# Three small groups of fp32 matrix products moved to sub-tiles of the systolic array, in a decoder layer on one core

## The chip, the cores and the metric

The kernel runs on one core of one Trainium2 chip. TensorE multiplies matrices (in the profile PE for the products and PEld for the loading of their stationary operand, the weights), VectorE (DVE), ScalarE (ACT) and GpSimd (POOL) do elementwise work, SyncE (SP) issues most of the transfers. SBUF is the on-chip memory with 128 partitions; products land in PSUM, from where VectorE and ScalarE fetch them. The metric is the device time of one execution in microseconds; lower is better.

## The reference, cut to what matters

One decoder layer on 256 tokens of width 2048, all in float32: a projection feeds a gated DeltaNet (8 heads of 128) and an attention branch (8 heads); both are merged, projected, and followed by a gated feed-forward of width 5632. The change touches the DeltaNet:

```python
h = rms_norm(x, ln1[l])
proj = h @ w_in[l]
qkv_a, beta_a, decay_a, z_a, ... = split_columns(proj)
...
q = l2norm(q.reshape(shp))        # x * rsqrt(sum(x * x) + 1e-6)
...
beta = jax.nn.sigmoid(beta_logit)
g = -jnp.exp(a_log) * jax.nn.softplus(a_logit + dt_bias)
...
a_mat = jnp.where(strict, jnp.einsum('bhncd,bhnsd->bhncs', kb, k) * gamma, 0.0)
t_mat = lax.linalg.triangular_solve(eye + a_mat, eye, left_side=True, lower=True, unit_diagonal=True)
u = jnp.einsum('bhncs,bhnsv->bhncv', t_mat, v * beta[..., None])
```

Three things in it matter here: the 16 columns of the projection that give `beta_a` and `decay_a` (called gate columns below), the sum of squares of q over the head, and the inverse `t_mat` of a unit lower triangular matrix. The kernel takes chunks of 128 tokens instead of 64, which gives the same function.

## The kernel before, in words

All large products run on TensorE as a stream of 128x128 weights times 256 or 512 columns: `main_mm` (L98) issues them, `load_w` fetches a block of weights and splits it into a high and a low part of type fp32r with one cast on ScalarE (L108) and one subtraction on VectorE (L105). In order, the projections are q, k and v of the DeltaNet (`ps_gdn`), its output gate (`ps_z`), v of the attention (`ps_v`), q and k of the attention (`ps_moba`), the branch gates (`ps_gate`), then the branch outputs, the output projection, up and down.

Everything else is background work, written as Python generators in the list `bg`. `main_mm` counts up estimated nanoseconds, and each time they pass `EVERY` = 1700 it calls `tick()` (L90), which takes every generator one `yield` further. So a `yield` in the code stands for about 1.7 us of projections between two steps. A scheduler that simulates the engines then fixes the order of the instructions on each engine; each engine works through its own list in order. PSUM has three buffers for projections and five (`sdt`, tag "sd") for the background.

The touched places:

- *Gate columns* (L299 to L310). The weights `wbd` (128 x 16 columns of 16) are split into a high part in columns 0 to 15 and a low part in columns 32 to 47 of `wb2`; the gap is cleared by GpSimd. The normalised input stands in two fp32r parts `hh`, `hl`, so 16 x 2 products of 48 weight columns by 256 tokens add up in `ps_bd`. Rows 0 to 15 and 32 to 47 are then added to `z0`.
- *Sums of squares of q* (L497 to L501, in `gdn_pair`, which runs four times, for two heads each time). GpSimd squares q into `sq`. For two heads and two halves of the tokens, a product has `sq` as weights and one column of `ones` as stream, so that the sums land as columns, one lane per token. VectorE adds epsilon, scales, and writes row 0 of `st` (`S(0)`), which is read at the end of the unit (L659).
- *Inverse by doubling* (L596 to L627, in `gdn_unit`, twice, for 8 matrices of 128x128 each). First the 32x32 diagonal blocks are inverted on VectorE, into `TL` and, transposed, into `U`. Then two levels, w = 32 and w = 64, join neighbouring blocks: Y = (off-diagonal block of A) x (inverse of the upper block), then the new off-diagonal block of the inverse is -(inverse of the lower block) x Y. Each level does this with full 128x128 products: 8 of them (`py`) with the whole of `ats[p]` as weights and 64 columns as stream, a multiplication on VectorE with a 0/1 mask `my` into the even column blocks of Y, whose odd column blocks GpSimd had cleared, then 8 products (`pu`), and a subtraction from U on VectorE. A yield stands after the clearing of Y, after the mask, and after the subtraction.

An fp32 product is written as one `pe.matmul` and shows as two matmuls in the profile.

Of the kernel before, what the change touches and what calls it, by code (L numbers as in the profile page):

```python
# [11 lines left out]
F32 = mybir.dt.float32  # L12
F32R = mybir.dt.float32r
I32 = mybir.dt.int32
AF = mybir.ActivationFunctionType
ALU = mybir.AluOpType
# [3 lines left out]
P = 128  # L20
T = 256
D = 2048
KD = D // P
# [4 lines left out]
EPS = 1e-6  # L28
# [1 line left out]
SHIFT = 72  # L30
ATT_SCALE = 128 ** -0.5
CONST_FIELDS = [
    ("ident", 128), ("nm", 128), ("my", 2 * 64), ("nm3", 3 * 128), ("invf", 16),
]


def const_array():
    c = {}
    i = np.arange(P)
    c["ident"] = np.eye(P)  # L40
    c["nm"] = np.where(i[None, :] >= i[:, None], 0.0, -30000.0)
    my = np.zeros((P, 2, 64))
    for j in range(2):
        m = 32 << j
        e = i[(i // m) % 2 == 0][None, :]
        my[:, j, :] = (i[:, None] // (2 * m) == e // (2 * m)) & ((i[:, None] // m) % 2 == 1)
    c["my"] = my
    nm3 = np.zeros((P, 3, P))
    nm3[:, 1:, :] = np.where(i[None, :] <= i[:, None], 0.0, -1e30)[:, None, :]
    c["nm3"] = nm3  # L50
    inv = np.float32(500000.0) ** (-np.arange(16, dtype=np.float32) / np.float32(16))
    c["invf"] = np.broadcast_to(inv, (P, 16))
    return np.concatenate([c[n].reshape(P, -1) for n, _ in CONST_FIELDS], axis=1).astype(np.float32)
# [17 lines left out]
def layer_kernel(ctx: ExitStack, tc: tile.TileContext, xT, pos, cst, ceye, vec, convw, ffw, bdv,  # L71
                 w_gdn, w_z, w_bd, w_moba, w_mv, w_gate, w_ba, w_bb, w_o, w_up, w_dn, fnorm, out):
    nc = tc.nc
    pe, act, dve, pool, sp = nc.tensor, nc.scalar, nc.vector, nc.gpsimd, nc.sync
# [5 lines left out]
    def r3(t, b):  # L80
        return t.rearrange("p (a b) -> p a b", b=b)

    def mmg(ps, pairs, start=True, stop=True, **kw):
        n = len(pairs)
        for i, (a, b) in enumerate(pairs):
            pe.matmul(ps, a, b, start=(start and i == 0), stop=(stop and i == n - 1), **kw)  # L86
# [17 lines left out]
    def low(hi, lo, src, eng=None):  # L104
        return (eng or dve).tensor_tensor(lo, src, hi.bitcast(F32), op=ALU.subtract)  # L105
# [29 lines left out]
    ln1v, ln2v, gnv = vc[:, 0:16], vc[:, 16:32], vc[:, 32:33]  # L135
    ones = keep.tile([P, P + 96], F32, name="ones")[:, :P]
# [20 lines left out]
    def sdt(name):  # L157
        return pst[1].tile([P, 512], F32, name=name, tag="sd")
# [58 lines left out]
    def rstd(parts, tp, name):  # L217
        ps = sdt(name)[:, :T]
        mmg(ps, [(ones, t) for t in parts])
        r = tp.tile([P, T], F32, name=name)  # L220
        act.activation(r, ps, AF.Sqrt, bias=epst, scale=1.0 / D)
        dve.reciprocal(r, r)
        return r
# [7 lines left out]
    hh, hl = hc[:, :, 0, :], hc[:, :, 1, :]  # L231
# [3 lines left out]
    g = n1.enter_context(tc.tile_pool(name="n1", bufs=1, side="right"))  # L235

    xs = g.tile([P, KD, T], F32, name="xs")
# [15 lines left out]
    for k0, n in steps:  # L253
        s = slice(k0, k0 + n)
        for b in range(2):
            w = r3(wq[b], P)[:, s]
# [9 lines left out]
    wbd = g.tile([P, KD, 16], F32, name="wbd")  # L266
# [8 lines left out]
    C, o = {}, 0  # L275
# [1 line left out]
        C[n] = ct[:, o:o + s]  # L277
        o += s
    ident, nm = C["ident"], C["nm"]
    my = r3(C["my"], 64)  # L280
    eye = fk.tile([P, 8, 32], F32, name="eye")
    sp.dma_start(eye, ceye)

# [3 lines left out]
    sq = []  # L287
# [8 lines left out]
    dve.tensor_tensor(sq[0][:, 0], sq[0][:, 0], sq[0][:, 1], op=ALU.add)  # L296


    wb2 = g.tile([P, KD, 48], F32R, name="wb2")  # L299
    pool.memset(wb2.bitcast(F32), 0.0)  # L300
    act.copy(wb2[:, :, 0:16], wbd)
    low(wb2[:, :, 0:16], wb2[:, :, 32:48], wbd)
    s = sdt("ps_bd")[:48, :T]
    mmg(s, [(wb2[:, k, :], x_[:, k, :]) for k in range(KD) for x_ in (hh, hl)])
    R1 = rstd([sq[0][:, 0, :]], fk, "R1")
    R1b = both(R1)
    beta = fk.tile([16, T], F32, name="beta")
    z0 = fk.tile([16, T], F32, name="z0")
    act.copy(z0, s[32:48, :])
    dve.tensor_tensor(z0, z0, s[:16, :], op=ALU.add)  # L310
    ea = fk.tile([16, 1], F32, name="ea")
    gc = fk.tile([16, T], F32, name="gc")
    rem = fk.tile([16, P], F32, name="rem")
# [9 lines left out]
    m = m_st.enter_context(tc.tile_pool(name="m", bufs=2, reuse_waits="tile"))  # L323
    gdn_st, gu_st = ExitStack(), ExitStack()
    dr = gu_st.enter_context(tc.tile_pool(name="dr", bufs=2, space=bass.MemoryType.DRAM))
    gu = gu_st.enter_context(tc.tile_pool(name="gu", bufs=1, reuse_waits="tile"))
    g = gdn_st.enter_context(tc.tile_pool(name="g", bufs=2, side="right", reuse_waits="tile"))
# [124 lines left out]
    def wait(n):  # L452
        for _ in range(n):
            yield
# [17 lines left out]
    def gdn_pair(u, pr, kq, v):  # L472
# [9 lines left out]
        sq = g.tile([P, 2, T], F32, name="sqq", tag="un", bufs=1)  # L482
# [11 lines left out]
        def S(r):  # L494
            return st[:, r, 4 * pr:4 * pr + 4]

        pq = r3(sdt("ssq")[:, :4], 1)  # L497
        for i in range(2):
            for j in range(2):
                pe.matmul(pq[:, 2 * i + j], sq[:, j, i * P:(i + 1) * P], ones[:, :1], start=True, stop=True)  # L500
        dve.tensor_scalar(S(0), pq[:, :, 0], EPS, P * EPS, op0=ALU.add, op1=ALU.mult)  # L501

        pg = u["gB"][:, 2 * pr:2 * pr + 2, :]
        gam = g.tile([P, 2, 3, P], F32, name="gam", bufs=1)
        for j in range(2):
            c = 8 + hs[j]
            dve.scalar_tensor_tensor(gam[:, j, 0, :], pg[:, j, :P], cols[:, 0, c:c + 1], nm,
                                     op0=ALU.subtract, op1=ALU.min)
            dve.tensor_scalar(gam[:, j, 1, :], pg[:, j, P:], cols[:, 2, c:c + 1], 0.0, op0=ALU.add, op1=ALU.min)
            dve.scalar_tensor_tensor(gam[:, j, 2, :], pg[:, j, P:], cols[:, 1, c:c + 1], nm,  # L510
                                     op0=ALU.subtract, op1=ALU.min)
        act.activation(gam, gam, AF.Exp)
        yield

        kqh = g.tile([P, 2, 2, T], F32R, name="kqh", bufs=1)
        kql = g.tile([P, 2, 2, T], F32R, name="kql", bufs=1)
# [10 lines left out]
        jk = g.tile([P, P], F32, name="jk", bufs=1)  # L527
# [8 lines left out]
        for j in range(2):  # L536
            h, e = 2 * pr + j, 4 * pr + j
# [3 lines left out]
        for j in range(2):  # L541
            h, e = 2 * pr + j, 4 * pr + 2 + j
# [4 lines left out]
        for i in range(2):  # L547
            for k in range(4):
                b = slice(32 * k, 32 * k + 32)
# [9 lines left out]
        if pr:  # L559
            yield from gdn_unit(u)  # L560

    def gdn_unit(u):
# [4 lines left out]
        ats = [aq[:, 0, 2 * a + j, 2 * i, :] for a in range(2) for i in range(2) for j in range(2)]  # L567

        def half(t, i):
            return t.rearrange("p (a i j) c -> p i a (j c)", i=2, j=2)[:, i]  # L570


        N = gu.tile([P, 32, 32], F32, name="N", tag="Y", bufs=1)
        pool.dma_start(N.rearrange("p m c -> p (m c)"), bass.AP(tensor=dN.tensor, offset=dN.offset, ap=[[1024, 32], [0, 4], [1, 1024]]))
# [15 lines left out]
        TL = gu.tile([P, 8, P], F32, name="TL", tag="u", bufs=1)  # L590
        pool.dma_start(TL, dT[:, :P].rearrange("p s c -> s p c"))
        yield from wait(12)
        U = gu.tile([P, 8, P], F32, name="U", tag="U", bufs=1)
        with tc.issue_after(lows[-1].ins):
            dve.transpose(U.rearrange("p a b -> p (a b)"), TL.rearrange("p a b -> p (a b)"))
        for lv in range(2):  # L596
            w = 32 << lv

            def even(t):
                return t.rearrange("p a (b c d) -> p a b c d", c=2, d=w)[:, :, :, 0, :]  # L600

            def odd(t):
                return t.rearrange("p a (b c d) -> p a b c d", c=2, d=w)[:, :, :, 1, :]

            if lv == 0:
                Tm = even(TL)
            else:

                t21 = gu.tile([32, 8, 32], F32, name="t21", tag="Tm", bufs=1)
                dve.transpose(t21, U[:32, :, 32:64])  # L610
                pool.dma_start(TL[32:64, :, :32], t21)
                yield from wait(2)
                Tm = TL[:, :, :64]
            Y = gu.tile([P, 8, P], F32, name="Y", tag="Y", bufs=1)
            pool.memset(odd(Y), 0.0)
            yield
            py = sdt("py").rearrange("p (a b) -> p a b", a=8)
            for p in range(8):
                pe.matmul(py[:, p], ats[p], Tm[:, p], start=True, stop=True)  # L619
            dve.tensor_tensor(even(Y), py.rearrange("p a (b d) -> p a b d", d=w),  # L620
                              my[:, lv:lv + 1, :].rearrange("p a (b d) -> p a b d", d=w).to_broadcast([P, 8, 64 // w, w]), op=ALU.mult)
            yield
            pu = sdt("pu").rearrange("p (a b) -> p a b", a=8)
            for p in range(8):
                pe.matmul(pu[:, p], Y[:, p, :], odd(U)[:, p], start=True, stop=True)  # L625
            dve.tensor_tensor(odd(U), odd(U), pu.rearrange("p a (b d) -> p a b d", d=w), op=ALU.subtract)
            yield  # L627
        x = gu.tile([P, 8, P], F32, name="x", tag="u", bufs=1)
        pairs = [(2 * a + j, 4 * a + j) for a in range(2) for j in range(2)]
# [24 lines left out]
        act.copy(half(ot, 1), po.rearrange("p (a j) c -> p a (j c)", j=2))  # L654
        so = gu.tile([P, 8, P], F32, name="so", tag="Y", bufs=1)
        pool.tensor_tensor(so, ot, ot, op=ALU.mult)
# [9 lines left out]
        for p in range(8):  # L666
            dve.scalar_tensor_tensor(o2[:, p // 4 * 4 + p % 2 * 2 + p // 2 % 2, :], ot[:, p, :], st[:, 7, p:p + 1], zv[:, p, :],
                                     op0=ALU.mult, op1=ALU.mult)
        done.add(("out", u["n"]))
        yield from turn(zv, o2.rearrange("p a c -> p (a c)"), gu.tile([P, 8, P], F32, name="ox", tag="Y", bufs=1), sp, 4, 1)  # L670
        yield from wait(2)
# [113 lines left out]
    for n in range(2):  # L785
# [6 lines left out]
        for a in range(2):  # L792
            ps = by_token(w_moba[8 * n + 4 * a:8 * n + 4 * a + 4], hc, KD, "ps_moba")
            t = (m if a else mq).tile([P, 4, 2, P], F32, name=f"qk{a}", bufs=1)
# [27 lines left out]
    for t, nm_ in ((ya, "a"), (yb, "b")):  # L822
        yc.append(yp.tile([P, H, 2, T], F32R, name="yc" + nm_))
        for i in range(4):
            s = slice(2 * i, 2 * i + 2)
# [6 lines left out]
    m = m_st.enter_context(tc.tile_pool(name="mp", bufs=1, reuse_waits="tile"))  # L832
# [53 lines left out]
    b = bp.enter_context(tc.tile_pool(name="b", bufs=2, reuse_waits="tile"))  # L886
    sqa = b.tile([P, 2, T], F32, name="sqa", bufs=1)
    h2 = hp.tile([P, KD, 2, T], F32R, name="h2", tag="hc")
    for c in range(8):
# [10 lines left out]
        if c % 2 == 0:  # L900
            s = slice(2 * c, 2 * c + 4)
# [7 lines left out]
        else:  # L909
            sq = b.tile([P, 2, T], F32, name="sq2")  # L910
# [14 lines left out]
    b = bk.enter_context(tc.tile_pool(name="b2", bufs=2, reuse_waits="tile"))  # L925
# [69 lines left out]
    for k in range(NF):  # L995
        last = k >= NF - LAST
        ab = LAST if last else 2
        if k == NF - LAST:
# [3 lines left out]
            b = bk.enter_context(tc.tile_pool(name="b3", bufs=2, reuse_waits="tile"))  # L1002
# [102 lines left out]
```

## Time and profile before

| | us |
|---|---|
| median of three timed runs | 1457.8 (1457.72 to 1457.9) |
| profiled execution, whole | 1458.26 |
| profiled execution, span | 1456.5 |
| TensorE busy in the span | 1444.5 |
| VectorE / ScalarE / GpSimd busy | 953.1 / 739.7 / 106.3 |
| granted TensorE clock, mean | 0.998 |

The span goes from the first to the last instruction of the trace. A row of a group names the line, the engine, the operation, output<-inputs, the shape and the number, then busy time and the mean of one. "Busy" of a matmul is modelled and overlaps with that of its neighbours; what a matmul costs is read from the distance between starts. In the chain that ended last, a row is the start, the length and the instructions of one stretch.

### The profile page before, as it was taken

Reading aid. Unit: us, or ns where it says so; the run is one execution under the profiler, and the core shown is the slowest. Engines: PE = TensorE matmul, PEld = TensorE weight load, DVE = VectorE, ACT = ScalarE, POOL = GpSimd, SP = SyncE. Lnnn points to the kernel's source line nnn. Section 1 sums busy time; section 2 is a strip of 40 time slices with the busy share of each in tenths; the row PEclk is TensorE's granted clock in tenths of the full one; section 3 lists DMA queues with packets and bytes.
Section 4 is the critical chain, followed back from the end, with each engine's and each line's share of the span. In section 5 each row is a group of like instructions: output and inputs, shape, how many; then the busy total and the mean of one; then the engine's idle time right before and its main releaser. Section 6 shows DMA issues by size and latency. Waiting matters only on the chain.

```text
span 1456.5 us, 19062 instructions
## 1 busy us (share of the span) xinstructions
PE 1444.5 (99%) x7193; PEld 1227.7 (84%) x7193; DVE 953.1 (65%) x1358; ACT 739.7 (51%) x944; POOL 106.3 (7%) x121
## 2 busy tenths in 40 slices
PE   8999999999999999999999999999999999999997
PEld 8898899888888888888888888888888888888886
DVE  7987876888455446767656676676666567655554
ACT  5665444645365443435445555455455455444444
POOL 0011000110001110001100011110011000000000
PEclk9999999999999999999999999999999999999999
DMA  9466554577535555676557787677677667555552
GB/s 334 165 214 212 185 191 130 162 222 244 181 139 189 202 189 193 216 264 226 180 178 233 176 255 224 196 247 233 185 253 237 210 210 249 183 194 202 187 189 86
DMA packets 206252, 297.43 MB, mean 204 GB/s; under 512 B 167272, under 2 KB 169712, under 8 KB 174032
## 3 DMA queue, kind: packets, MB, share of 16 engines
q1 hardware_dynamic: 185952, 288.27, 60.0%
q10 hardware_dynamic: 18128, 4.20, 1.4%
q0 software_dynamic: 2080, 3.75, 0.8%
q8 instruction: 56, 0.92, 0.3%
q14 instruction: 36, 0.29, 0.1%
HBM read 273.54 MB, written 3.15 MB: 190 GB/s over the span
## 4 chain that ended last, share of the span: by engine, by line
PE 97%; DMA 2%; SPq 0%; DVE 0%; ACT 0%; issue 0%; DVEq 0%; ACTq 0%
PE ps_up L98 33%; PE pd L98 16%; PE ps_gate L98 12%; PE ps_gdn L98 9%; PE ps_moba L98 6%; PE ps_br L98 6%; PE ps_wo L98 5%; PE ps_z L98 3%; PE ps_v L98 3%; DMA wraw<-in_w_gdn 1%; DMA x<-in_xT 1%; PE g L86 1%; PE pu L625 0%; PE py L619 0%; PE ps_bd L86 0%; PE po L86 0%
## 5 line engine op out<-in xcount | busy, mean ns | idle before, releaser
L105 DVE TENSOR_TENSOR wl<-wraw,wh 128x1024 fp32r<-128x1024 f32 x496 | 595.9, 1235 | 317.9 <-ACT wh L108 314.0
L108 ACT CAST wh<-wraw 128x1024 fp32r<-128x1024 f32 x496 | 495.9, 1047 | 459.3 <-PE ps_up L98 181.1
L98 PE MATMUL ps_up<-wh,h 128*128 128x512 f32 x1408 | 433.6, 389 | 0.0
L98 PEld LDWEIGHTS ps_up<-wh,h 128*128 128x128 f32 x1408 | 264.2, 188 | 54.7
L98 PE MATMUL ps_up<-wl,h 128*128 128x512 f32 x704 | 274.0, 389 | 0.0
L98 PE MATMUL ps_gate<-wh,hc 128*128 128x512 f32 x512 | 157.1, 391 | 0.0
L98 PEld LDWEIGHTS ps_up<-wl,h 128*128 128x128 f32 x704 | 132.1, 188 | 27.5
L98 PE MATMUL pd<-wl,ah 128*128 128x512 f32 x336 | 129.5, 389 | 0.0
L98 PE MATMUL pd<-wh,al 128*128 128x512 f32 x336 | 129.1, 389 | 0.0
L98 PE MATMUL ps_gdn<-hc,wh 128*128 128x256 f32 x704 | 125.6, 281 | 0.0
L98 PEld LDWEIGHTS ps_gate<-wh,hc 128*128 128x128 f32 x512 | 95.8, 188 | 19.4
L98 PEld LDWEIGHTS ps_gdn<-hc,wh 128*128 128x128 f32 x704 | 107.9, 188 | 0.3
L98 PE MATMUL ps_gdn<-hc,wl 128*128 128x256 f32 x352 | 98.5, 280 | 0.7 <-DVE wl L105 0.7
L98 PE MATMUL ps_gate<-wl,hc 128*128 128x512 f32 x256 | 97.8, 391 | 0.0
L98 PE MATMUL pd<-wh,ah 128*128 128x512 f32 x336 | 92.5, 389 | 0.0
L98 PE MATMUL ps_wo<-mc,wh 128*128 128x512 f32 x256 | 89.2, 391 | 0.2 <-DVE mc L865 0.2
L98 PE MATMUL ps_moba<-wh,hc 128*128 128x512 f32 x256 | 77.8, 390 | 0.0
L958 POOL TENSOR_TENSOR acts<-sgt,cvf 128x256 f32<-128x256 f32 x44 | 40.8, 932 | 478.3 <-DVE cvf L941 478.3
L98 PEld LDWEIGHTS pd<-wh,ah 128*128 128x128 f32 x336 | 63.1, 188 | 13.4 <-ACT ut L970 0.3
L98 PEld LDWEIGHTS pd<-wh,al 128*128 128x128 f32 x336 | 63.0, 188 | 13.2
L98 PEld LDWEIGHTS pd<-wl,ah 128*128 128x128 f32 x336 | 63.1, 188 | 13.1
L108 ACT CAST ah<-acts 128x256 fp32r<-128x256 f32 x44 | 17.6, 406 | 109.6 <-PE pd L98 109.6
(428 smaller groups left out, 1713.7 us busy)
## 6 DMA issues: line engine op xcount, KB each, us to landing
wraw<-in_w_up SPq DMA_DIRECT2D x88, 1024.0 KB, 7.2
wraw<-in_w_dn SPq DMA_DIRECT2D x44, 1024.0 KB, 4.9
wraw<-in_w_gate SPq DMA_DIRECT2D x32, 1024.0 KB, 5.0
wraw<-in_w_gdn SPq DMA_DIRECT2D x22, 1024.0 KB, 4.9
wraw<-in_w_moba SPq DMA_DIRECT2D x16, 1024.0 KB, 5.5
wraw<-in_w_o SPq DMA_DIRECT2D x16, 1024.0 KB, 5.4
uc<-xt SPq DMA_DIRECT2D x352, 32.0 KB, 2.0
wraw<-in_w_z SPq DMA_DIRECT2D x8, 1024.0 KB, 6.4
```

What stands on the lines that cost most here:

```text
L86: pe.matmul(ps, a, b, start=(start and i == 0), stop=(stop and i == n - 1), **kw)
L98: pe.matmul(ps, a, b, start=start, stop=stop, skip_group_check=True)
L105: return (eng or dve).tensor_tensor(lo, src, hi.bitcast(F32), op=ALU.subtract)
L108: casts.append(act.copy(hi, src))
L958: pool.tensor_tensor(acts[:, ch, :], gates[c][:, k, :], t, op=ALU.mult)
```

## The change

The products of the three places become smaller ones that use only a part of the array: where the weights stand in 32 or 64 partitions, a part of its rows, and where they have few columns, a group of 32 of its columns, chosen by the partitions of PSUM that the product writes.

- Gate columns: `wbd` is multiplied in place by the norm's weights; the products take `wbd` and the raw input `xs` in fp32, 16 weight columns each, in turn into partitions 0, 32, 64 and 96 of `ps_bd`. The four partial sums are added into `z0`. `wb2`, its clearing, its cast and its subtraction go.
- Sums of squares: `ones` (32 columns) is now the weight and `sq` the stream; each of the four sums lands as rows in its own 32 partitions, 32 times the same. VectorE adds epsilon and scales all of it into `qs` (in the buffer of `jk`), and after the yield a transpose and a copy of every 32nd column bring it to `S(0)`.
- Doublings: only the blocks themselves are multiplied. At w = 32 a product has 32x32 weights and 32 columns, two for each matrix; at w = 64 64x64 weights and 64 columns, one for each. Y has only the blocks, so it is not cleared and not masked; it is copied, and the result is written to U with its sign turned. The constant `my` goes.

The number of yields stays the same.

```diff
 CONST_FIELDS = [
-    ("ident", 128), ("nm", 128), ("my", 2 * 64), ("nm3", 3 * 128), ("invf", 16),
+    ("ident", 128), ("nm", 128), ("nm3", 3 * 128), ("invf", 16),
 ]
...
-    wb2 = g.tile([P, KD, 48], F32R, name="wb2")
-    pool.memset(wb2.bitcast(F32), 0.0)
-    act.copy(wb2[:, :, 0:16], wbd)
-    low(wb2[:, :, 0:16], wb2[:, :, 32:48], wbd)
-    s = sdt("ps_bd")[:48, :T]
-    mmg(s, [(wb2[:, k, :], x_[:, k, :]) for k in range(KD) for x_ in (hh, hl)])
+    dve.tensor_tensor(wbd, wbd, ln1v[:, :, None].to_broadcast([P, KD, 16]), op=ALU.mult)
+    s = sdt("ps_bd")[:, :T]
+    for k in range(KD):
+        r = 32 * (k % 4)
+        pe.matmul(s[r:r + 16], wbd[:, k, :], xs[:, k, :], start=(k < 4), stop=(k >= KD - 4))
...
-    act.copy(z0, s[32:48, :])
-    dve.tensor_tensor(z0, z0, s[:16, :], op=ALU.add)
+    act.copy(z0, s[:16, :])
+    for r in (32, 64, 96):
+        dve.tensor_tensor(z0, z0, s[r:r + 16, :], op=ALU.add)
...
-        pq = r3(sdt("ssq")[:, :4], 1)
+        pq = sdt("ssq")
         for i in range(2):
             for j in range(2):
-                pe.matmul(pq[:, 2 * i + j], sq[:, j, i * P:(i + 1) * P], ones[:, :1], start=True, stop=True)
-        dve.tensor_scalar(S(0), pq[:, :, 0], EPS, P * EPS, op0=ALU.add, op1=ALU.mult)
+                c = 32 * (2 * i + j)
+                pe.matmul(pq[c:c + 32, :P], ones[:, :32], sq[:, j, i * P:(i + 1) * P], start=True, stop=True)
+        qs = g.tile([P, P], F32, name="qs", tag="jk", bufs=1)
+        dve.tensor_scalar(qs, pq[:, :P], EPS, P * EPS, op0=ALU.add, op1=ALU.mult)
...
         act.activation(gam, gam, AF.Exp)
         yield
+        pe.transpose(pq[:, P:2 * P], qs, ident)
+        dve.tensor_copy(S(0), pq[:, P:2 * P:32])
...
-            Y = gu.tile([P, 8, P], F32, name="Y", tag="Y", bufs=1)
-            pool.memset(odd(Y), 0.0)
-            yield
-            py = sdt("py").rearrange("p (a b) -> p a b", a=8)
+            Y = gu.tile([P, 8, w], F32, name="Y", tag="Y", bufs=1)
+            yield
+            py = sdt("py").rearrange("p (a b) -> p a b", a=8)[:, :, :w]
+            pu = sdt("pu").rearrange("p (a b) -> p a b", a=8)[:, :, :w]
+            spans = [(slice(e, e + w), slice(e + w, e + 2 * w)) for e in range(0, P, 2 * w)]
             for p in range(8):
-                pe.matmul(py[:, p], ats[p], Tm[:, p], start=True, stop=True)
-            dve.tensor_tensor(even(Y), py.rearrange("p a (b d) -> p a b d", d=w),
-                              my[:, lv:lv + 1, :].rearrange("p a (b d) -> p a b d", d=w).to_broadcast([P, 8, 64 // w, w]), op=ALU.mult)
-            yield
-            pu = sdt("pu").rearrange("p (a b) -> p a b", a=8)
+                for e, o in spans:
+                    pe.matmul(py[o, p], ats[p][e, o], TL[e, p, e], start=True, stop=True)
+            for e, o in spans:
+                dve.tensor_copy(Y[o], py[o])
+            yield
             for p in range(8):
-                pe.matmul(pu[:, p], Y[:, p, :], odd(U)[:, p], start=True, stop=True)
-            dve.tensor_tensor(odd(U), odd(U), pu.rearrange("p a (b d) -> p a b d", d=w), op=ALU.subtract)
+                for e, o in spans:
+                    pe.matmul(pu[e, p], Y[o, p], U[o, p, o], start=True, stop=True)
+            for e, o in spans:
+                dve.tensor_scalar(U[e, :, o], pu[e], -1.0, None, op0=ALU.mult)
             yield
```

More of the change, by code (lines that the diff above doesn't have):

```diff
@@ L41, in const_array @@
     c["nm"] = np.where(i[None, :] >= i[:, None], 0.0, -30000.0)
[L42 to L47, printed above, removed]
     nm3 = np.zeros((P, 3, P))
@@ L279, in layer_kernel @@
     ident, nm = C["ident"], C["nm"]
-    my = r3(C["my"], 64)
     eye = fk.tile([P, 8, 32], F32, name="eye")
@@ L597, in gdn_unit @@
             w = 32 << lv
[L599 to L607, printed above, removed]
+            if lv == 1:
                 t21 = gu.tile([32, 8, 32], F32, name="t21", tag="Tm", bufs=1)
@@ L612, in gdn_unit @@
                 yield from wait(2)
-                Tm = TL[:, :, :64]
-            Y = gu.tile([P, 8, P], F32, name="Y", tag="Y", bufs=1)
-            pool.memset(odd(Y), 0.0)
+            Y = gu.tile([P, 8, w], F32, name="Y", tag="Y", bufs=1)
             yield
-            py = sdt("py").rearrange("p (a b) -> p a b", a=8)
+            py = sdt("py").rearrange("p (a b) -> p a b", a=8)[:, :, :w]
+            pu = sdt("pu").rearrange("p (a b) -> p a b", a=8)[:, :, :w]
+            spans = [(slice(e, e + w), slice(e + w, e + 2 * w)) for e in range(0, P, 2 * w)]
             for p in range(8):
-                pe.matmul(py[:, p], ats[p], Tm[:, p], start=True, stop=True)
-            dve.tensor_tensor(even(Y), py.rearrange("p a (b d) -> p a b d", d=w),
-                              my[:, lv:lv + 1, :].rearrange("p a (b d) -> p a b d", d=w).to_broadcast([P, 8, 64 // w, w]), op=ALU.mult)
+                for e, o in spans:
+                    pe.matmul(py[o, p], ats[p][e, o], TL[e, p, e], start=True, stop=True)
+            for e, o in spans:
+                dve.tensor_copy(Y[o], py[o])
             yield
-            pu = sdt("pu").rearrange("p (a b) -> p a b", a=8)
             for p in range(8):
-                pe.matmul(pu[:, p], Y[:, p, :], odd(U)[:, p], start=True, stop=True)
-            dve.tensor_tensor(odd(U), odd(U), pu.rearrange("p a (b d) -> p a b d", d=w), op=ALU.subtract)
+                for e, o in spans:
+                    pe.matmul(pu[e, p], Y[o, p], U[o, p, o], start=True, stop=True)
+            for e, o in spans:
+                dve.tensor_scalar(U[e, :, o], pu[e], -1.0, None, op0=ALU.mult)
             yield
```

## The prediction

> **What bounds the kernel now.** I read the page's first two lines, then its chain that ended last, then the waits of TensorE.
>
> ```profile
> span 1456.5 us, 19062 instructions
> PE 1444.5 (99%) x7193; PEld 1227.7 (84%) x7193; DVE 953.1 (65%) x1358; ACT 739.7 (51%) x944; POOL 106.3 (7%) x121
> PE 97%; DMA 2%; SPq 0%; DVE 0%; ACT 0%; issue 0%; DVEq 0%; ACTq 0%
> PE ps_gdn L261 <- DMA xs<-in_xT: 1.3, 2, 0.7
> PE warm L242 <- POOL ones L137: 1.0, 1, 1.0
> PE ps_gdn L98 <- DVE wl L105: 0.7, 1, 0.7
> PE ps_gdn L261 <- DVE hc L214: 0.5, 1, 0.5
> PE ps_wo L98 <- DVE mc L865: 0.2, 1, 0.2
> ```
>
> TensorE is busy for 1444.5 of 1456.5 us and makes 97% of the chain; all its waits sum to 3.7 us, and none is for an instruction that the diff touches. So a microsecond of TensorE's stream taken out anywhere after the start is a microsecond of the span, and one added is paid in full. What VectorE, ScalarE and GpSimd do counts only if TensorE comes to wait for it. The profiled execution took 1458.26 us, 1.76 us around its span and 0.46 us over the median of the three timed runs, 1457.8. I work out a difference against the trace and put it on that median.
>
> The touched blocks, from the chain in order of time (start, length, what; one of the four blocks of py, pu and ssq each), and how their weights and passes look:
>
> ```profile
> 34.19 3.64 PE ps_bd L86 x32
> 120.70 0.79 PE ssq L500 x8
> 203.41 1.73 PE py L619 x16
> 208.85 1.73 PE pu L625 x16
> 329.20 0.43 PE sc L738 x2
> 329.64 0.22 PE sc L739 x2
> 341.21 0.11 PE pT L760
> ...
> L86 PEld LDWEIGHTS ps_bd<-hc,wb x32: 120/121/122, 33.9 to 37.4; 128*48 128x48 f32 x32
> L98 PEld LDWEIGHTS ps_up<-wh,h 128*128 128x128 f32 x1408 | 264.2, 188 | 54.7
> ...
> 368.13 1.87 PEld L619 LDWEIGHTS py<-TL,aq 128*128 128x128 f32 x16
> 369.92 0.19 PEld L98 LDWEIGHTS ps_gate<-wh,hc 128*128 128x128 f32 x1
> ```
>
> A block of py holds 8 products of fp32 and shows 16 matmuls: an fp32 product is two passes, each with its own weight load. One block of py or pu has 16 passes in 1.73 us, 108 ns each, though only 64 columns stream; the loads follow one another at (369.92 - 368.13)/16 = 112 ns. These blocks go at the pace of loading 128 columns of weights. Streaming alone is shown by sc: 256 columns of fp32 in 0.43/2 = 215 ns a pass, 128 columns in 110 ns, so 0.84 ns a column. All touched blocks together take 3.64 + 4 x 0.79 + 8 x 1.73 = 20.6 us; the change can't win more than that, and wins far less.
>
> **What a small pass costs.** No row shows a load of 32 or 64 columns. A load of 48 columns lasts 121 ns and one of 128 columns 188 ns: 0.84 ns a column. Taking 96 columns (81 ns) or 64 columns (54 ns) off the spacing of 112 ns leaves 31 ns a pass for w = 32 and 58 ns for w = 64; streaming at 0.84 ns gives 27 and 54 ns, less than that. This is the low end. The other end is the shortest spacing that the trace shows:
>
> ```profile
> 78.54 0.28 PE L98 MATMUL ps_gdn<-hc,wh 128*128 128x256 f32 x1
> 78.75 0.14 PEld L423 LDWEIGHTS pt_cols<-ct,gc 16*128 16x128 f32 x1
> 78.81 0.14 PEld L424 LDWEIGHTS pt_cols<-ct,beta 16*128 16x128 f32 x1
> 79.00 0.14 PEld L425 LDWEIGHTS pt_cols<-ct,rem 16*128 16x128 f32 x1
> 79.16 1.05 PE L500 MATMUL ssq<-ones,sqq 128*128 128x1 f32 x8
> ...
> 86.49 22.41 PE ps_gdn L98 x192
> ...
> L619 PEldq EVENT_SEMAPHORE  x1: 51/51/51, 387.3 to 387.3; - x1
> 391.54 1.73 PE py L619 x16
> ```
>
> Five transposes of 16 rows follow at (79.00 - 78.75)/4 = 62.5 ns. I take 31 and 58 ns, not 62.5, for two reasons. Those five load 128 columns each, so 62.5 ns may be their load. And the sequencer runs well ahead: for py at 391.54 it passed a semaphore at 387.3, 4.2 us earlier, so a burst of 32 passes comes largely out of a filled queue. The 62.5 ns stay as the high end. The Trainium skill (TensorE: Matmul & The Clock Gate, section Back-to-back issue gap) gives a floor of about 25 ns between small matmuls, and about 62 ns where each is decoded in microcode; no run here shows which of the two holds.
>
> **The price of a visit to a smaller tile.** The same rows show what it costs to leave 128 x 128 work for a smaller part of the array and return. From the last ps_gdn to the first ssq pass are 0.62 us; one ps_gdn pass is 22.41/192 = 0.117 and five transposes are 0.31, so 0.19 us are left over, about half at each end. The change makes 13 such visits (1 for the gate columns, 4 for ssq, 8 for py and pu): 2.5 us. The Trainium skill speaks against the change here (TensorEngine Tiling (Array Packing), section Key Properties): switching the tiling mode drains TensorE, changing only the tile does not. The trace agrees with the first half, at 0.19 us a visit; by the second half, the changes of group inside a visit are free, which no run here shows.
>
> **The change part by part.**
>
> Gate columns: 32 passes of 48 x 256 (3.64 us) go; 16 fp32 products, 32 passes of 16 x 256, come, one in each column group in turn. TensorE takes matmuls in order, and a product's second pass needs its own group, so only this overlap is open: the second pass of one product beside the first pass of the next. That is 17 x 0.215 = 3.66 us, plus a visit 3.85, so **+0.2**. Bounds: +3.4 if nothing overlaps (32 x 0.215 = 6.88, plus 0.19), 0 if the visit is free.
>
> Sums of squares: 8 passes at the pace of loading sq as weights (0.79) become 4 products with 128 streamed columns, 5 x 0.11 = 0.55 with the same overlap, a visit 0.19, and a transpose of 0.11 one yield later: 0.85, **+0.06 in each of 4 pairs, +0.2**. Bounds: +0.38 each without overlap (8 x 0.11), -0.13 with a free visit.
>
> Level w = 32: 8 full products become 16 of 32 x 32, 32 passes: 32 x 0.031 + 0.19 = 1.18 against 1.73, **-0.55 in 4 blocks, -2.2**. Bounds: +0.46 each at 62.5 ns; -1.05 each if the two diagonal blocks also run beside each other and the visit is free.
>
> Level w = 64: 16 passes of 64 x 64, 16 x 0.058 + 0.19 = 1.12, **-0.61 in 4 blocks, -2.4**. At 62.5 ns, -0.54 each.
>
> Around it:
>
> ```profile
> L620 DVE TENSOR_TENSOR Y<-py,ct x4: 685/690/692, 205.3 to 393.4; 128x512 f32<-128x512 f32 x4
> 38.26 0.41 DVE L310 TENSOR_TENSOR z<-z,ps_bd 16x256 f32<-16x256 f32 x1 [0.20 <-ACT z L309]
> 40.05 1.75 DVE L222 RECIPROCAL R<-R 128x256 f32<-128x256 f32 x1 [1.28 <-ACT R L221]
> ...
> 285.52 0.49 PE L86 MATMUL g<-kqh 128*128 128x512 f32 x1
> 286.06 0.15 DVE L501 TENSOR_SCALAR st<-ssq 128x4 f32<-128x4 f32 x1
> ...
> 238.81 0.79 PE ssq L500 x8
> 254.22 0.12 DVE L501 TENSOR_SCALAR st<-ssq 128x4 f32<-128x4 f32 x1
> ...
> 84.34 0.28 DVE L509 TENSOR_SCALAR gam<-gB,cols 128x128 f32<-128x128 f32 x1
> ```
>
> VectorE's copies and negations have the same element counts per lane as the masked product (690 ns) and the subtraction, split in two 32-row halves at w = 32 (about 0.41 us each, the row of 16 x 256): some +0.1 us a step, on an engine 65% busy, with at least one yield (about 1.7 us of TensorE's work) ahead of the reader. The two extra additions for z0, 0.8 us, fit the 1.28 us in which VectorE waits ahead of the reciprocal. GpSimd's clearing of Y and ScalarE's cast of the gate weights go; TensorE waited for neither. The smaller constants take 64 KB off the loads at the start: nothing counted, 0.2 us at most. The new wait is the transpose's, for qs on VectorE: all of TensorE's queue stands behind it, the projection first. The old row L501 came 0.5 us after ssq had ended, and 128 x 128 costs 0.28 us where it cost 0.15; the yield between covers that. In the third pair it came 14.6 us late; by the order of the code it had to follow the first unit's last use of st, a buffer that qs does not share, so there only the small copy behind the transpose comes late, and nobody on TensorE waits for that. Without that cover it is some 0.5 us a pair, 2 us in all.
>
> **Sum:** +0.2 + 0.2 - 2.2 - 2.4 = -4.2 us; 1457.8 - 4.2 = **1453.6 us**.
>
> **The rivals.** A measurement of this kernel can tell about 0.2%, 2.9 us, from no change.
>
> - *Short passes go no faster than 62.5 ns.* For it: no shorter spacing stands in the trace. Against: the sequencer's lead. Level 32 then loses 4 x 0.46, level 64 still wins 4 x 0.54: in sum +0.1, 1457.9 us.
> - *The column groups don't run side by side* (the change doesn't do what it says). For it: no row shows two matmuls beside each other. Then the gate columns pay +3.4 and ssq 4 x 0.38, against -4.6: +0.3, 1458.1 us. Here the Trainium skill speaks for the change (TensorE: Matmul & The Clock Gate, section Part 3: Packing small matmuls): matmuls in different tiles start some 4 ns apart, and strictly in order. No run here shows it.
> - *Slower: every change of group inside a visit drains the array.* Half of the 0.19 us would be paid at each step from one group to the next: 16 for the gate columns, 16 for ssq, 64 at level 32, 96 in all. At 0.095 us that is 9.1 us, 1462.7 us. It makes the kernel slower by 0.2% from (4.2 + 2.9)/96 = 0.074 us a step. For it: both ends of the only visits seen cost this. Against: there the number of rows in use changed too.
> - *More is won:* the two diagonal blocks of level 32 overlap (another 4 x 0.5) and visits are free (2.5): 1449.1 us.
>
> **How the numbers follow.** Forecast 0.44 (own range 1452 to 1455.3, of which 0.06 lies within 0.2%), 62.5 ns 0.17, no overlap 0.13 (0.04 of it above 0.2%, with stalls at the transposes), drains at each step 0.13, more won 0.13. Faster: 0.38 + 0.13 = 0.51; within: 0.06 + 0.17 + 0.09 = 0.32; slower 0.17. The range 1450 to 1461 leaves out the lower half of the last case (0.06) and most of the drains (0.10).
>
> **What would show it.** In the chain of the changed kernel: py and pu blocks of 32 passes near 1.0 us and of 16 near 0.93; ps_bd near 3.7 us; ssq near 0.55, its transpose 0.11 with no wait of TensorE for qs. A ps_bd near 6.9 means no overlap, one near 2 a fourfold one; a level-32 block near 2 us means the floor of 62.5 ns, one above 2.5 drains. A new row in TensorE's waits, or long stretches of the projections spaced otherwise than 0.117 us, would mean that the order of the work moved, for which I count nothing.

## The result, and the profile after

| | before | after |
|---|---|---|
| median of the timed runs, us | 1457.76 (1457.43 to 1457.9, 4 runs) | 1450.39 (1449.9 to 1451.11, 4 runs) |
| ratio, 95% interval | | 0.995 (0.9935 to 0.9965) |
| profiled execution, us | 1458.26 | 1451.11 |

The changed kernel is 7.4 us faster; forecast were 4.2. A difference of less than about 2 us between two kernels with four runs each lies within the uncertainty of such a ratio. First the head of the page of the changed kernel and TensorE's waits (engine, line and what waited, what for: us in total, times, longest).

```profile
span 1449.3 us, 19191 instructions
PE 1436.5 (99%) x7261; PEld 1214.1 (84%) x7261; DVE 956.0 (66%) x1368; ACT 736.6 (51%) x941; POOL 102.0 (7%) x116
```

```profile
PE ps_gdn L255 <- DMA xs<-in_xT: 2.3, 3, 1.1
PE warm L236 <- POOL ones L131: 1.0, 1, 1.0
PE ps_gdn L92 <- DVE wl L99: 0.5, 1, 0.5
PE ps_gate L92 <- ACT gts L804: 0.5, 1, 0.5
PE ps_wo L92 <- DVE mc L855: 0.2, 1, 0.2
```

TensorE still sets the time: 8.0 us less busy, 7.2 us less span. No row waits for `qs`, which the new transpose needs. One row is new, `ps_gate` on ScalarE's `gts`; it comes up again below. This table holds TensorE's products only; its weight loads (PEld) wait by themselves, and they come up below too.

The touched blocks on TensorE's timeline of the changed kernel (start, length, what; equal instructions are merged into one row, whose length runs to the modelled end of the last):

```profile
33.91 1.92 PE L296 MATMUL ps_bd<-xs,wbd 128*16 128x256 f32 x32
35.76 0.70 PE L80 MATMUL R<-sq,ones 128*128 128x256 f32 x2
...
118.90 0.42 PE L494 MATMUL ssq<-sqq,ones 128*32 128x128 f32 x8
119.25 0.50 PE L80 MATMUL g<-kqh 128*128 128x512 f32 x1
...
214.44 1.14 PE L608 MATMUL py<-TL,aq 64*64 64x64 f32 x16
215.51 0.39 PE L92 MATMUL ps_gdn<-hc,wl 128*128 128x256 f32 x1
```

and the doublings of the second unit in its chain that ended last:

```profile
369.89 0.62 PE py L608 x32
375.95 0.62 PE pu L614 x32
389.04 1.07 PE py L608 x16
395.78 1.07 PE pu L614 x16
```

From its first pass to the next block (35.76 - 33.91) `ps_bd` takes 1.85 us where it took 3.64; the level w = 32 takes 0.62 and w = 64 takes 1.07 where both took 1.70 from the first pass to the next block (1.73 as the chain shows them). Merged rows hide how the passes stand to each other, so here are the distances between successive starts in the changed kernel, from the trace, in ns:

```
ps_bd, 32 passes:   7 7 6 207  6 7 6 197  6 7 6 197  6 7 6 197  5 8 6 196  6 8 6 196  6 8 5 197  6 7 6
ssq, 8 passes:      7 7 6 114  6 7 7
py, w = 32, start:  7 45  7 25  7 25  6 25  7 25  7 25  6 25  7 25 ...
py, w = 64:         107 58 59 58 58 59 58 58 59 58 58 59 58 58 59
```

`ps_bd` runs in eight steps of four passes that start within 20 ns, some 216 ns apart: all four column groups work at once. `ssq` takes two such steps. At w = 32 the two diagonal blocks run as a pair, 32 ns a pair; at w = 64, where the two passes of a product share one tile, one pass follows another at 58 ns. The change of group, 7 ns, is nearly free. (Records don't name the group, so which pass stands in which step is inferred.)

I then compared the start of the same work in both traces. Behind `ps_bd` the projections gain 1.60 us; at the four pairs `ssq` with its transpose gains 0.37, 0.28, 0.34 and 0.41; the blocks of w = 32 gain 0.97, 0.62 (a projection falls into the middle of this one), 0.98 and 0.98; those of w = 64 0.52, 0.51, 0.53 and 0.53. That is 8.64 us. The spans differ by 7.2, so more than one microsecond is given back. The changed kernel's starts have four gaps among the projections that the kernel before hasn't: 511 ns at 293.48 us, 499 at 323.38, 840 at 434.23 and 466 at 456.56, where two starts are usually 228 apart. The rows of the weight loads behind three of them:

```profile
293.99 0.19 PEld L92 LDWEIGHTS ps_moba<-wl,hc 128*128 128x128 f32 x1 [0.55 <-DVE wl L99]
323.85 0.30 PEld L728 LDWEIGHTS sc<-qk,qk 128*128 128x128 f32 x2 [0.50 <-issue]
457.03 0.19 PEld L92 LDWEIGHTS ps_gate<-wl,hc 128*128 128x128 f32 x1 [0.50 <-DVE wl L99]
```

Two waited for VectorE's `wl`, the low part of a block of weights, which came late; for the one at 323 us the profile names nothing. The fourth and largest, on TensorE's timeline and on ScalarE's:

```profile
434.23 0.39 PE L92 MATMUL ps_gate<-wl,hc 128*128 128x512 f32 x1
435.07 0.73 PE L92 MATMUL ps_gate<-wh,hc 128*128 128x512 f32 x2 [0.45 <-ACT gts L804]
```

```profile
429.22 1.28 ACT L650 ACT_TABLE_LOAD   x1
430.51 0.21 ACT L650 ACTIVATE st<-st 128x8 f32<-128x8 f32 x1
430.74 1.28 ACT L737 ACT_TABLE_LOAD   x1
...
433.04 1.28 ACT L804 ACT_TABLE_LOAD   x1
434.33 0.69 ACT L804 ACTIVATE gts<-ps_gate,cols 128x512 f32<-128x512 f32 x1
```

The sigmoid that empties the projection's PSUM buffer (L804) stands behind three loads of a function table, 1.28 us each, one of them for a square root that fell between two exponentials. The kernel before has the same three loads, but there they are spread out, with a cast and a copy between the second and the third, and no gap on TensorE:

```profile
431.82 1.28 ACT L660 ACT_TABLE_LOAD   x1
433.11 0.21 ACT L660 ACTIVATE st<-st 128x8 f32<-128x8 f32 x1
433.34 1.28 ACT L747 ACT_TABLE_LOAD   x1
...
435.53 1.99 ACT L108 CAST wh<-wraw 128x1024 fp32r<-128x1024 f32 x2
438.78 0.48 ACT L762 COPY pT__4052<-pT 128x384 f32<-128x384 f32 x1 [1.26 <-PE pT L760]
439.28 1.28 ACT L814 ACT_TABLE_LOAD   x1
440.57 0.69 ACT L814 ACTIVATE gts<-ps_gate,cols 128x512 f32<-128x512 f32 x1
```

So there were two questions: how far column groups overlap and what sets it, and whether the order of the work really gave time back.

### The profile page after: what moved, and what is told of

It is laid out like the page before. It is cut to its first block, busy times and chain, and to the rows that moved or that the text cites. A ratio compares the mean times of both kernels' runs of the same rounds, so it can differ in the third digit from the quotient of the medians.

```text
span 1449.3 us, 19191 instructions
## 1 busy us (share of the span) xinstructions
PE 1436.5 (99%) x7261; PEld 1214.1 (84%) x7261; DVE 956.0 (66%) x1368; ACT 736.6 (51%) x941; POOL 102.0 (7%) x116
## 4 chain that ended last, share of the span: by engine, by line
PE 77%; ACT 1%; SPq 1%; DVE 0%; issue 0%; DMA 0%; DVEq 0%; ACTq 0%
PE ps_up L92 33%; PE pd L92 17%; PE ps_gate L92 10%; PE ps_wo L92 6%; PE ps_br L92 6%; PE ps_moba L92 4%; SPq L457 1%; PE sc L728 0%; DVE wl L99 0%; ACT wh L102 0%; PE py_b L757 0%; DMA ya<-ox 0%; PE po L80 0%; PE sc L729 0%; PE pu L614 0%
```

## Experiments: the three parts by themselves

**Gate columns alone**, on the kernel before: only these lines of the change.

```diff
-    mmg(s, [(wb2[:, k, :], x_[:, k, :]) for k in range(KD) for x_ in (hh, hl)])
+    for k in range(KD):
+        r = 32 * (k % 4)
+        pe.matmul(s[r:r + 16], wbd[:, k, :], xs[:, k, :], start=(k < 4), stop=(k >= KD - 4))
...
```

> Gate columns alone, all else as before. The changed kernel's trace shows ps_bd in 1.85 us where it took 3.64, and all projections behind it 1.60 us earlier. If the gains are those of the blocks on TensorE, this kernel is 1.6 us faster than before (1456.2), within 0.3. If the order that the scheduler chooses matters as much as the blocks, it lies anywhere from 1455 to 1458. By the prediction on record (only the second pass of one product beside the first of the next) it would be 0.2 us slower.

Measured: 1455.88 us against 1457.87, ratio 0.9987 (0.9978 to 0.9997). The trace shows -1.60 us at `ps_bd`, -0.64 at the first loads, and then nothing up to 656 us, where a gap of the kernel before is 0.11 shorter. The first loads differ between kernels that begin alike: at the same place, 23 us, the changed kernel stands at -0.21, the later kernel without the sums of squares at +0.13 and a later one that copies `gts` at -0.92. So what stands at the first loads isn't shown to come from the edits. The part that I had put at +0.2 wins.

**Sums of squares alone:**

```diff
-                pe.matmul(pq[:, 2 * i + j], sq[:, j, i * P:(i + 1) * P], ones[:, :1], start=True, stop=True)
+                c = 32 * (2 * i + j)
+                pe.matmul(pq[c:c + 32, :P], ones[:, :32], sq[:, j, i * P:(i + 1) * P], start=True, stop=True)
...
```

> Sums of squares alone. In the changed kernel's trace the projections gain 0.28 to 0.41 us at each of the four pairs, transposes included. Blocks alone: 1.4 us faster than before (1456.4). Order: 1455 to 1458. The prediction on record had 0.2 us slower.

Measured: 1457.15 us, ratio 0.9995 (0.9986 to 1.0005): no difference that could be told. The four pairs do win 0.40, 0.24, 0.35 and 0.43 us, 1.42 in all; but a gap of 843 ns between starts came up at 440.80 us, which the kernel before hasn't:

```profile
440.80 0.39 PE L98 MATMUL ps_gate<-wl,hc 128*128 128x512 f32 x1
441.65 0.73 PE L98 MATMUL ps_gate<-wh,hc 128*128 128x512 f32 x2 [0.46 <-ACT gts L818]
```

It is the same wait as in the changed kernel, more than 150 us behind the last edited product (the fourth pair, near 285 us): no edited instruction takes part in it, but the order around it had moved.

**Doublings alone:**

```diff
-                pe.matmul(py[:, p], ats[p], Tm[:, p], start=True, stop=True)
+                for e, o in spans:
+                    pe.matmul(py[o, p], ats[p][e, o], TL[e, p, e], start=True, stop=True)
...
```

> Doublings alone. In the changed kernel's trace a level-32 block gains 0.98 us (0.62 where another projection got into it) and a level-64 block 0.52. Blocks alone: 4 x 0.98 + 4 x 0.52 = 6.0 us faster (1451.8). If the stalls that the changed kernel has between 293 and 457 us (1.7 us in four places) come with the doublings, 4 to 5 us (1453 to 1454). The prediction on record had 4.6 us.

Measured: 1452.01 us, ratio 0.9961 (0.9946 to 0.9976), -5.9 us. The profiled executions lie 6.4 apart, with -0.66 at the first loads, -2.62 in the first unit, -2.8 behind it, another -0.35 at 656 us where a gap of the kernel before is gone, and no new gap. The parts sum to 2.0 + 0.7 + 5.9 = 8.6 us; the whole is 7.4. The first two parts are known to about 1.4 us only, the third and the whole to about 2.2, so this sum by itself doesn't show a loss.

## Experiments: what lets column groups overlap

**Four products in a row on one group** (AAAABBBBCCCCDDDD in place of ABCD four times), the changed kernel otherwise:

```diff
-        r = 32 * (k % 4)
+        r = 32 * (k // 4)
...
```

> The changed kernel with one edit: four consecutive products of the gate columns go to the same column group before the next group's turn (the sums are the same). If TensorE takes passes in the order of the code and only neighbours on different groups run beside each other, nearly nothing overlaps: ps_bd takes 6.3 to 6.9 us (32 passes of 0.215) where it took 1.85, and the time is 1455 us. If it picks passes for a free group out of a window of some dozens, ps_bd stays near 1.9 us and the time at 1450.4.

TensorE's timeline of this kernel:

```profile
33.98 4.54 PE L296 MATMUL ps_bd<-xs,wbd 128*16 128x256 f32 x32
38.45 0.70 PE L80 MATMUL R<-sq,ones 128*128 128x256 f32 x2
```

4.47 us to the next block: neither serial (32 x 0.215 = 6.9) nor all side by side (1.9). By the starts there are 20 steps of some 215 ns: four with one pass, twelve with two, four with one. So a group's fifth pass starts together with the next group's first. A single run took 1454.19 us, 3.8 over the changed kernel; 2.6 of that are in this block (4.47 - 1.85).

**The two diagonal blocks one after the other** at w = 32:

```diff
-            for p in range(8):
-                for e, o in spans:
+            for e, o in spans:
+                for p in range(8):
...
```

> The changed kernel with the loops of the level-32 products swapped: all eight matrices of one diagonal block, then all eight of the other. The run of four (e4) showed passes of a later group starting only when at most three held-back passes stood before them. If that window of three is right, a level-32 block of 32 passes goes in 28 steps of some 30 ns (0.84 to 0.9 us) where it went in 16 (0.50 from first to last start), 1.4 us more over four blocks. With strict order it would be 31 steps (0.93 to 1.0), with a window of dozens 16 steps (0.50).

The chain of this kernel, second unit:

```profile
369.47 1.02 PE py L608 x32
375.93 1.02 PE pu L614 x32
```

1.02 us where the alternating order takes 0.62, with passes 32 ns apart and four pairs at the change of block: 28 steps in place of 16. So the speed of level 32 comes from the order in which the products are issued. The time of the whole, 1451.14 us in a single run, is too near to 1450.4 to say more.

**Two products in a row on one group** (AABBCCDD twice). I had explained the last two by one common window in which three passes may be held back, and that asks for 11 steps here.

```diff
-        r = 32 * (k % 4)
+        r = 32 * (k // 2 % 4)
...
```

> The changed kernel with the gate columns' products in pairs on one group (AABBCCDDAABBCCDD). A window of three held-back passes gives 11 steps of about 0.21 us: 2.1 to 2.4 us from the first to the last start plus one step (8 steps and 1.54 in the changed kernel). A window of two gives 14 steps (2.7 to 3.0), four gives 10 (1.9 to 2.1), strict order 25 (5.0 to 5.4).

```profile
34.41 1.95 PE L296 MATMUL ps_bd<-xs,wbd 128*16 128x256 f32 x32
36.28 0.70 PE L80 MATMUL R<-sq,ones 128*128 128x256 f32 x2
```

The common window fell: 1.87 us to the next block, eight steps of four passes, as with ABCD; only the four starts of a step are 13 ns apart and not 7. What fits all four patterns is a short queue for **each** column group: one pass runs and three wait; passes are handed out in program order, and that stops only when the next pass's own group is full.

**A forecast from that**, AAABBBCCCDDDABCD:

```diff
-        r = 32 * (k % 4)
+        r = 32 * (k // 3 if k < 12 else k - 12)
...
```

> The gate columns in the order of groups AAABBBCCCDDDABCD in place of ABCD four times; all else as in the changed kernel. Theory, a queue for each column group with one pass running and three waiting, filled in program order and blocked only when the next pass's own group is full: 14 steps of about 0.215 us in place of 8, with passes of D starting before the last of B, so ps_bd goes from about 1.9 us to about 3.2 us, and the time rises by about 1.3 us. With two waiting passes 17 steps (3.8 us), with four 11 steps (2.5 us). Rival, one common window of three held-back passes: 18 steps, about 4.0 us. Rival, strictly in order, a pass only beside its predecessor: 32 passes less the overlaps at 15 changes of group, 28 steps or fewer but well over 20, over 4.5 us.

(The 18 steps given there for the common window are a miscount; counted through they are 15.) The timeline and, below, the starts of `ps_bd` in ns, one step in each bracket:

```profile
33.71 3.24 PE L296 MATMUL ps_bd<-xs,wbd 128*16 128x256 f32 x32
36.88 0.70 PE L80 MATMUL R<-sq,ones 128*128 128x256 f32 x2
```

```
[0] [226] [442 448] [657 673] [873 889 895] [1088 1105 1122] [1321 1338 1343] [1537 1553 1570]
[1769 1786 1792 1798] [1985 2002 2018 2024] [2201 2217] [2416 2433] [2649] [2864]
```

Fourteen steps, 3.17 us, with 1, 1, 2, 2, 3, 3, 3, 3, 4, 4, 2, 2, 1, 1 passes: step for step what a queue of three waiting passes for each group gives (two would give 17 steps, four 11). If passes had to start in program order, the same count gives 25. So passes of different groups overtake each other. The time of a single run, 1451.83 us, is 1.4 over the changed kernel; its block is 1.32 longer.

## Experiments: what the moved order costs

**Without the sums of squares:** the changed kernel with the old products for them put back, that is, gate columns and doublings alone.

```diff
+                pe.matmul(pq[:, 2 * i + j], sq[:, j, i * P:(i + 1) * P], ones[:, :1], start=True, stop=True)
-                c = 32 * (2 * i + j)
-                pe.matmul(pq[c:c + 32, :P], ones[:, :32], sq[:, j, i * P:(i + 1) * P], start=True, stop=True)
...
```

> The kernel before with the gate columns and the doublings of the change, the sums of squares left as they were. The parts measured alone sum to -8.6 us (-2.0, -0.7, -5.9), the whole change to -7.4, and the sums of squares alone won 1.4 us in their blocks and gave 0.84 back in a stall of ps_gate for ScalarE's gts near 440 us. Theory: the 0.84 us stall near 434 us in the changed kernel comes with the order of ScalarE's work and not with the sums of squares as such; without them the time is that of the whole plus about 1.4 us if the stall stays (1451.8 us), and about 0.6 us above the whole if it goes (1451.0 us). Rival, that the parts simply add: 1457.8 - 2.0 - 5.9 = 1449.9 us, faster than the whole change, with no stall of ps_gate for gts.

TensorE's waits in this kernel:

```profile
PE ps_gdn L255 <- DMA xs<-in_xT: 1.9, 3, 0.9
PE warm L236 <- POOL ones L131: 1.0, 1, 1.0
PE ps_gdn L92 <- DVE wl L99: 0.7, 1, 0.7
PE ps_wo L92 <- DVE mc L851: 0.2, 1, 0.2
```

Measured: 1450.18 us (ratio 0.9951, 0.9936 to 0.9966), the changed kernel's time within the uncertainty. Of the four gaps one is left (498 ns, at 324.45 us), and no wait for `gts`. The rival, that the parts add, gave 1449.9 and was nearer. So one third of the change wins 1.40 us in its blocks and nothing that shows in the time; a difference of 1.4 us can't be excluded at this uncertainty.

**Another spacing of the background steps**, `EVERY` 1600 and 1900 in place of 1700:

```diff
-EVERY = 1700
+EVERY = 1600
...
```

> The changed kernel with a background step every 1600 estimated ns instead of 1700; the work is the same. If the changed kernel's stalls on TensorE (840 ns at 434 us, and some 0.3 us each at 293, 323 and 456) are an accident of where the background falls, they shift or go: 1449 to 1452. If they belong to the new blocks, they stay where the blocks are and the time is 1450.4 within 0.3.

> The same with 1900 ns. In its order on ScalarE the square root of the second unit no longer stands between two exponentials ahead of the gates' eviction, so the stall of 840 ns at 434 us should be gone: about 1449.5 if nothing else moves, 1449 to 1452 by accident of place.

1600: 1450.58 us (ratio 0.9957, 0.9942 to 0.9972); the gaps became 1045 ns at 323 us, 846 at 434, 888 at 457 and 752 at 631. Three of the changed kernel's four stayed where they had been, none of them at a new block, so this run doesn't decide between the two accounts. 1900: 1456.6 us (ratio 0.9992, 0.9982 to 1.0002), well outside the 1449 to 1452 expected; the gap at 434 is gone, but others came, the largest here on TensorE's timeline:

```profile
326.33 0.39 PE L92 MATMUL ps_moba<-wh,hc 128*128 128x512 f32 x1
329.59 0.67 PE L728 MATMUL sc<-qk,qk 128*128 128x256 f32 x2 [2.88 <-DMA qk<-xt]
```

Behind it, `sc` waited 2.88 us for a transfer of `qk`. The same products lie some 6 us apart in time by their order alone: nearly as much as the whole change.

**Taking the gap away where it arises.** VectorE copies `gts` out of PSUM, and ScalarE puts it through the sigmoid in place, so that the PSUM buffer no longer waits for ScalarE's tables:

```diff
-            act.activation(gts[c // 4][:, i, c % 4, :], ps[i], AF.Sigmoid, scale=cols[:, 5 + i, 0:1])
+            t = gts[c // 4][:, i, c % 4, :]
+            dve.tensor_copy(t, ps[i])
+            act.activation(t, t, AF.Sigmoid, scale=cols[:, 5 + i, 0:1])
```

> The changed kernel, but the branch gates (gts) are first copied out of PSUM by VectorE and then put through the sigmoid by ScalarE in place, so that the buffer of PSUM does not wait for ScalarE's table loads. Theory, the start gap of 0.84 us near 434 us is a wait for the table loads in front of gts on ScalarE: it goes, and with it some 0.6 us of the time, 1449.8 us, if nothing else gets late. Rival, VectorE, which makes the low part of each weight block, gets 16 copies of about 0.55 us more (9 us) and the weights wl come late instead: new waits of TensorE for VectorE's wl at the branch gates, and no gain or a loss of up to 2 us.

TensorE's waits in this kernel, and the tile `gts` (duration min/median/max in ns, first and last start):

```profile
PE ps_gdn L255 <- DMA xs<-in_xT: 1.3, 1, 1.3
PE warm L236 <- POOL ones L131: 1.0, 1, 1.0
PE ps_wo L92 <- DVE mc L857: 0.2, 1, 0.2
```

```profile
L805 DVE COPY gts<-ps_gate x16: 673/691/692, 371.4 to 541.4; 128x512 f32<-128x512 f32 x16
L806 ACT ACTIVATE gts<-gts,cols x16: 716/722/725, 372.1 to 543.1; 128x512 f32<-128x512 f32 x16
```

Measured: 1448.95 us (1448.81 to 1449.78, 4 runs), ratio to the kernel before 0.9943 (0.9926 to 0.996): the lowest median of all, 1.4 under the changed kernel, though the two intervals overlap. More was won than expected: all four gaps are gone, and the same projections come earlier by 0.42, 0.32, 0.75 and 0.41 us at the four places, 1.9 in all; a gap of 422 ns at 646 us costs 0.3. Two of the four lie ahead of the first `gts` (371 us), so they were not waits for it; there the edit only moved the order again. Of the two behind it, the one at 456 us was, in the changed kernel, a wait for VectorE's `wl`; there VectorE had waited 6.45 us for ScalarE's cast, and ScalarE 4.38 us for a transfer before that. So by the reason given only the gap at 434 us, 0.75 of the 1.9 us, was to go. VectorE is 9 us busier (965.1 against 956.0), which cost nothing that shows.

The control: the same edit on the kernel before.

> The kernel before with the copy of gts by VectorE alone (the edit that took 1.4 us off the changed kernel). Theory: that edit only takes back the stalls that the change's moved order brought; the kernel before had none of them at the branch gates, so nothing is to be had there: 1457.6 us, within 0.5 us of the kernel before. Rival: the edit is worth as much without the change, 1456.2 us, and the changed kernel had given nothing back.

Measured: 1457.79 us against 1457.83, ratio 0.9999 (0.9989 to 1.0009). Where the gaps aren't, the edit is worth nothing that can be told. This fits the account that it won back on the changed kernel what the moved order had taken; the traces show the gaps gone, but the times of the two kernels alone are too near to each other to show what that was worth.

## Why the prediction was right, and where its sizes were not

The direction was right, for the reason given: TensorE's stream is the time, and what was taken out of it came off the span. The measured time lies in the range, but below the likeliest case's own range (1452 to 1455.3), between it and "more is won". Term by term, in us, the forecast and what the blocks gained in the trace:

| step | forecast | measured |
|---|---|---|
| gate columns | +0.2 | -1.60 |
| sums of squares, four pairs | +0.2 | -1.40 |
| level w = 32, four blocks | -2.2 | -3.55 |
| level w = 64, four blocks | -2.4 | -2.09 |
| order of the work | 0 | +1.9 and -0.25 |
| first loads | 0 | -0.21 |
| sum | -4.2 | -7.2 |

The -0.25 is a gap of 467 ns in the kernel before (at 655.78 us) that is gone. The -0.21 at the first loads isn't shown to belong to the change (see the first experiment). The sum is the difference of the two spans.

- *"Only this overlap is open: the second pass of one product beside the first pass of the next"* is the step that failed. It came from "TensorE takes matmuls in order". By the step counts it doesn't start them in order: up to three passes wait in front of each column group, others go past them, and with the groups in turn all four run at once. `ps_bd` has 8 steps instead of 17, `ssq` two instead of five. The Trainium skill (TensorE: Matmul & The Clock Gate, section Part 3: Packing small matmuls) has starts in different tiles some 4 ns apart, which the trace bears out with 7 ns, and strictly in order, which the 14 steps of AAABBBCCCDDDABCD contradict; the measurement decides.
- *Level w = 32: 32 passes of 31 ns* was the same mistake. The 31 ns were right for one pass behind another in one tile (32 in the blocks-in-a-row kernel), but two diagonal blocks share that time: 16 x 0.032 = 0.51 us instead of 0.99. The bound that allowed for it was -1.05 each, said to be with a free visit; but 16 x 0.031 + 0.19 - 1.73 = -1.05 has the visit paid, and without it the bound is -1.23. 0.98 came.
- *Level w = 64: 58 ns a pass* was exact. That the gain is 0.52 and not 0.61 has two reasons. The old block cost 1.70 us between starts, not the 1.73 of the chain's row, whose length runs to a modelled end; and the visit cost 1.70 - 0.93 - 0.52 = 0.25 us, not 0.19. Level 32 gives 1.70 - 0.51 - 0.98 = 0.21. The price was read off a visit that begins with transposes.
- *Transpose and `qs`:* as forecast, no wait of TensorE. The yield covered it.
- *The order of the work,* for which "I count nothing": the prediction named new rows in TensorE's waits as its sign, and one came. The four gaps took 1.9 of the 8.6 us. Here the prediction had luck: the overlap was underrated by 4.75 us (1.8 + 1.6 + 1.35) in three of the terms, and 1.65 of them went again by the order, which stood at nothing in the sum. Without that the time would have been about 1448.7 us, below the range of 1450 to 1461; the kernel without the four gaps measured 1448.95.

Of the rivals, the floor of 62.5 ns is refuted by 58 and 32 ns; "don't run side by side" by four starts within 20 ns; drains at each change of group by 7 ns, where that case had 95. (So the second half of the Trainium skill's rule that the prediction cites, that changing only the tile doesn't drain, is borne out.) "More is won" had the diagonal blocks right and the free visits wrong, and did not foresee the gate columns.

What stays open: why the scheduler's order puts these particular instructions together was not followed further, the gap at 323 us has no cause in the profile, and the depth of three was seen only in passes that use all 128 or 32 rows. That TensorE gets the products in the order of the code is assumed: the records name neither product nor group.

## What to carry to other kernels

Products in fp32 with few weight columns are worth trying in all four column groups, issued in turn (or at most two products in a row on one group): here they then ran four at a time, and the same products in runs of four took more than twice as long. What such an edit wins is read at its blocks, but what the kernel keeps is decided later: look for new gaps between TensorE's starts far behind the edit (over 150 us in one run here), and at what each stands behind, in the rows of the weight loads too: here one was an eviction behind ScalarE's table loads and two were weights that came late. Count a change that wins a microsecond as unproven until the kernel's own order has been tried with and without it.

## What the runs showed of the hardware that had not been expected

- The starts fit a short queue of its own for each column group, one pass running and three waiting: four patterns (8, 20, 8 and 28 steps) and one forecast (14 steps) come out of it step for step. Passes of different groups start 6 to 17 ns apart and not in program order.
- 32 x 32 fp32 products on two diagonal blocks went at 32 ns for two passes, 16 ns a pass on average.
- Entering and leaving a smaller tile cost 0.21 to 0.25 us a visit at the two levels of the inverse; changes of group within it about 7 ns.
